# A gated short-convolution block on one core: the output projection as 26 products instead of 7

## The chip, the cores and the metric

The kernel runs on one core of one Trainium2 chip. The metric is the device time of one execution in microseconds (us), from runs of the whole kernel; the profile is one execution taken by the hardware profiler. The engines are TensorE (PE, with its weight load PEld), VectorE (DVE), ScalarE (ACT), GpSimd (POOL) and SyncE (SP), the last of which here only issues transfers.

## What is computed

With x of 1024 rows and 1024 columns, all in float32:

```python
u = rms_norm(x, pre_norm)
z, bg, cg, v = split(u @ w_in, 4)                  # w_in: 1024 x 8192, four parts of 2048
y = bg * causal_dwconv(cg * v, conv_w) * silu(z)   # three taps, 2048 channels
m = y @ w_out                                      # w_out: 2048 x 1024
out = x + rms_norm(m, post_norm)
```

## The kernel before

A float32 product is made of three matmuls in a reduced-width float32 form: each operand is split into a high part (a rounding copy on ScalarE) and a low part (source minus high, on VectorE), and low x high, high x low and high x high are added in PSUM.

The input projection is done in groups of 128 columns. After a first chunk, the remaining 60 groups are taken in 20 triples (numbered 0 to 19). Each triple takes 20 products of block sums (`ORDER`), one after the other, 6 matmuls each; the weights' sums for the next triple are formed on GpSimd meanwhile (`sums`), split (`split_w`), and the products are read from PSUM into the groups (`read`). Convolution and gates follow as soon as their inputs are there (`run_due`), and `y_half` stores each half chunk of y (128 channels by 512 rows) to DRAM in `y_d`.

For the output projection the kernel uses 7 products a, b, c, e, d, f, g of 2x2 blocks. The sums of y that they need are made in DRAM during the main loop: `y_half` stores pieces also to `s_d`, and `more` adds further pieces there by accumulating transfers that GpSimd's queue issues. The sums of w_out are made the same way in `t_d` (`fetch_t`, `add_t`).

In the last stage (from line 908) `fetch_unit` loads 1 MB of y or w, `split_unit` splits it in two pieces of 128x1024 (ScalarE, then VectorE, lines 128 and 129, 851 and 852), `out_mm` runs the matmuls (lines 929 to 931: 4 row tiles q, 4 blocks k, 3 matmuls), and `combine` reads the products from PSUM. `early_half` and `finish_o` do the second normalisation and add x (`norm_square` at line 938, weighing at 953, 968 and 973, the reciprocal root in `rstd_finish` and `rstd_double`, final adds at 979 to 988). GpSimd's part in this stage is four subtractions at line 969 and one short add at the end. 18 buffers of 8 KB per partition (`up`) hold the split operands, 6 of 4 KB (`raw`) the loaded w. Instructions run on each engine in the order in which the program issues them.

Of the kernel before, what the change touches and what calls it, by code (L numbers as in the profile page):

```python
# [20 lines left out]
def kernel(
# [790 lines left out]
    OUT = [(i, h) for i in "abcedfg" for h in (0, 1)]  # L812
    UNITS_O = [(side, i, h) for i, h in OUT for side in "uy"]
    CQ = CH // 2
    fetched, OP = [], {}

    def fetch_unit():
        n = len(fetched)
        if n >= len(UNITS_O):
            return  # L820
        side, i, h = UNITS_O[n]
        js = slice(h * CQ, (h + 1) * CQ)
        far = slice(CH + h * CQ, CH + (h + 1) * CQ)
        if side == "u":
            plain_u = {"a": wov[:, js, :HB], "b": wov[:, far, :HB], "f": wov[:, far, HB:]}
            src = plain_u[i] if i in plain_u else t_d[:, TK[i], js]
            r = []
            for q in (0, 1):
                r.append(raw.tile([P, 2, HB], F32, tag="raw", name=f"r{side}_{i}{h}{q}"))
                nc.sync.dma_start(r[q], src[:, 2 * q : 2 * q + 2])  # L830
        else:
            plain_y = {"a": y_d[:, js, :HB], "b": y_d[:, far, :HB], "g": y_d[:, far, HB:]}
            src = plain_y[i] if i in plain_y else s_d[:, SK[i], js]
            t = up.tile([P, 2, 2, HB], F32, tag="u", name=f"r{side}_{i}{h}")
            nc.sync.dma_start(t.rearrange("p a b c -> p (a b) c"), src)
            r = [t[:, 0], t[:, 1]]
        fetched.append(r)

    def split_unit(delayed=False):
        n = len(OP)  # L840
        if n >= 2 * len(UNITS_O):
            return
        side, i, h = UNITS_O[n // 2]
        q = n % 2
        t = new_u(f"o{side}_{i}{h}{q}")
        src, hi, lo = flat(fetched[n // 2][q]), flat(t[:, 0]), flat(t[:, 1])
        if (side, i) == ("u", "c"):
            nc.scalar.mul(hi, src, -1.0)
            nc.vector.scalar_tensor_tensor(lo, src, -1.0, hi.bitcast(F32), op0=ALU.mult, op1=ALU.subtract)
        elif delayed:  # L850
            nc.scalar.copy(hi, src)
            low_us.append(lambda: nc.vector.tensor_sub(lo, src, hi.bitcast(F32)))
        else:
            split(src, hi, lo)
        OP[side, i, h, q] = t
# [211 lines left out]
```

## Time and profile before

| | |
|---|---|
| time, median of 3 runs | 767.53 us (767.28 to 768.38) |
| profiled execution, span from the first to the last instruction | 766.2 us |
| PE busy | 758.0 us (99%) |
| VectorE, ScalarE, GpSimd busy | 485.9, 452.5, 459.7 us |
| moved by DMA | 116.55 MB, mean 152 GB/s |

The profiled execution's own time is known as its span; the time of a run also has what lies around the span. A row of instructions names the line, the engine, the operation, what is written and read, the shape, then the total busy time and the mean of one, then the idle time just before and what ended it. A row of the timeline begins with start and duration in us.

### The profile page before, as it was taken

The page shows a single profiled execution, that of the slowest core. Times are in us where ns is not written, and L with a number is a line of the kernel's source. Part 1 is how long each engine was busy: PE and PEld are TensorE (multiplying, and loading weights), DVE is VectorE, ACT ScalarE, POOL GpSimd, SP SyncE. Part 2 cuts the span into 40 slices and gives each one's busy share as a digit, 9 for nine tenths or more (in the row PEclk, how much of TensorE's full clock was granted, in tenths as well). Part 3 has the DMA queues.
Part 4 walks back from the last instruction along what each step waited for, and adds up shares of the span by engine and source line. Part 5 has one row for each costly group of instructions (what it writes and reads, how often), then busy time and mean ns, then how long its engine had stood idle before and what let it go on. Part 6 is the DMA issues. An engine that isn't in the chain of part 4 may idle for free.

```text
span 766.2 us, 10006 instructions
## 1 busy us (share of the span) xinstructions
PE 758.0 (99%) x3386; PEld 627.4 (82%) x3386; DVE 485.9 (63%) x748; ACT 452.5 (59%) x881; POOL 459.7 (60%) x564
## 2 busy tenths in 40 slices
PE   9999999999999999999999999999999999999996
PEld 8888888888888888888888888888888888888885
DVE  5898776475656566656565664655566957545755
ACT  8869766557646665754666665666467735544531
POOL 0687979669676876976797796797765220000021
PEclk9999999999999999999999999999999999999999
DMA  9401335447356358165465556574545689754237
GB/s 327 142 1 64 102 97 155 133 110 191 86 154 152 94 116 213 40 183 122 134 153 128 122 151 152 124 182 98 132 97 168 205 281 373 277 189 173 79 123 261
DMA packets 103363, 116.55 MB, mean 152 GB/s; under 512 B 4696, under 2 KB 70544, under 8 KB 102288
## 3 DMA queue, kind: packets, MB, share of 16 engines
q1 hardware_dynamic: 94080, 99.13, 39.4%
q0 software_dynamic: 9216, 16.78, 14.0%
q8 instruction: 26, 0.43, 0.2%
q14 instruction: 25, 0.20, 0.1%
q10 hardware_dynamic: 16, 0.00, 0.0%
HBM read 97.02 MB, written 44.04 MB: 184 GB/s over the span
## 4 chain that ended last, share of the span: by engine, by line
PE 98%; DMA 0%; DVE 0%; ACT 0%; issue 0%; DVEq 0%
PE pX L132 8%; PE pX L134 8%; PE pX L133 8%; PE pY L132 7%; PE pY L134 7%; PE pY L133 7%; PE po_x L931 4%; PE po_x L930 4%; PE po_x L929 4%; PE pV L134 4%; PE pV L132 4%; PE pV L133 4%; PE pZ L134 2%; PE pW L134 2%; PE pW L132 2%; PE pZ L132 2%
## 5 line engine op out<-in xcount | busy, mean ns | idle before, releaser
L362 DVE TENSOR_TENSOR sn<-sn,pY 128x512 f32<-128x512 f32 x57 | 39.2, 687 | 56.4 <-PE pY L134 28.9
L969 POOL TENSOR_TENSOR res<-xr,res 128x512 f32<-128x512 f32 x4 | 6.9, 1736 | 105.4 <-DVE res L968 104.0
L338 POOL TENSOR_TENSOR g<-g,sn 128x512 f32<-128x512 f32 x29 | 40.1, 1390 | 42.2 <-ACT sn L336 35.4
L362 DVE TENSOR_TENSOR sn<-sn,pX 128x512 f32<-128x512 f32 x57 | 39.2, 688 | 33.5 <-PE pX L134 33.5
L311 POOL TENSOR_TENSOR g<-sn,g 128x512 f32<-128x512 f32 x23 | 29.9, 1298 | 47.5 <-DVE sn L360 47.5
L336 ACT ACTIVATE sn<-sn 128x512 f32<-128x512 f32 x24 | 15.2, 632 | 64.1 <-DVE sn L362 40.0
L356 ACT ACTIVATE sn<-pV 128x512 f32<-128x512 f32 x38 | 20.6, 596 | 48.0 <-PE pV L134 48.0
L320 POOL TENSOR_TENSOR g<-g,sn 128x512 f32<-128x512 f32 x20 | 28.2, 1411 | 19.2 <-DVE sn L362 18.9
L354 ACT COPY sn<-pZ 128x512 f32<-128x512 f32 x19 | 11.2, 588 | 46.6 <-PE pZ L134 46.6
L368 POOL DMA_DIRECT2D s_d<-s_d x24 | 19.8, 823 | 21.6 <-DMA s_d<-y_d 14.1
L178 POOL TENSOR_TENSOR raw<-raw 128x256 f32<-128x256 f32 x40 | 32.3, 918 | 0.0
L360 DVE TENSOR_TENSOR g<-pY,g 128x512 f32<-128x512 f32 x15 | 10.4, 692 | 30.7 <-PE pY L134 30.7
L183 POOL TENSOR_TENSOR raw<-e,raw 128x256 f32<-128x256 f32 x40 | 28.7, 739 | 1.6
L179 POOL TENSOR_TENSOR e<-raw,raw 128x512 f32<-128x512 f32 x20 | 26.2, 1312 | 1.6
L938 ACT ACTIVATE jk<-res 128x512 bf16<-128x512 f32 x12 | 7.6, 631 | 31.7 <-DVE res L1008 13.0
L132 PE MATMUL pp<-b,wn 128*128 128x512 f32 x62 | 24.6, 397 | 0.0
L133 PE MATMUL pp<-b,wn 128*128 128x512 f32 x62 | 24.3, 393 | 0.0
L134 PE MATMUL pp<-b,wn 128*128 128x512 f32 x62 | 24.2, 390 | 0.0
L301 DVE SCALAR_TENSOR_TENSOR g<-g,cw,cv 128x512 f32<-128x512 f32 x30 | 22.5, 749 | 1.7
L233 DVE TENSOR_TENSOR wE<-wE,wE 128x512 fp32r<-128x512 f32 x20 | 13.7, 686 | 14.1 <-ACT wE L232 14.0
L301 DVE SCALAR_TENSOR_TENSOR cv<-g,cw,cv 128x512 f32<-128x512 f32 x30 | 22.4, 747 | 0.0
L233 DVE TENSOR_TENSOR wC<-wC,wC 128x512 fp32r<-128x512 f32 x20 | 13.7, 687 | 11.9 <-ACT wC L228 11.9
(388 smaller groups left out, 2903.3 us busy)
## 6 DMA issues: line engine op xcount, KB each, us to landing
raw<-in_sc_w_in SPq DMA_DIRECT2D x64, 512.0 KB, 4.2
t_d<-in_sc_w_out SPq DMA_DIRECT2D x32, 256.0 KB, 4.6
s_d<-g SPq DMA_DIRECT2D x29, 256.0 KB, 2.1
s_d<-s_d POOLq DMA_DIRECT2D x24, 256.0 KB, 4.4
y_d<-g SPq DMA_DIRECT2D x23, 256.0 KB, 2.5
t_d<-in_sc_w_out POOLq DMA_DIRECT2D x16, 256.0 KB, 7.8
t_d<-t_d POOLq DMA_DIRECT2D x16, 256.0 KB, 4.8
xr<-in_x SPq DMA_DIRECT2D x8, 512.0 KB, 5.7
```

What stands on the lines that cost most here:

```text
L132: nc.tensor.matmul(ps, lo, u[:, 0, kk], start=first, stop=False, skip_group_check=True)
L133: nc.tensor.matmul(ps, hi, u[:, 1, kk], start=False, stop=False, skip_group_check=True)
L134: nc.tensor.matmul(ps, hi, u[:, 0, kk], start=False, stop=last, skip_group_check=True)
L178: 0: lambda: (add(w2[:, 0], w2[:, 0], w2[:, 1]), add(w2[:, 2], w2[:, 1], w2[:, 2])),
L183: 5: lambda: (sub(w0[:, 2], e[:, 3], w0[:, 2]), sub(w0[:, 0], e[:, 3], w0[:, 0])),
L301: nc.vector.scalar_tensor_tensor(g if j == TAPS - 1 else ps, g, tap(c, j), ps, op0=ALU.mult, op1=ALU.add)
L311: nc.gpsimd.tensor_mul(g, src, g)
L338: when([(c, "cv", h), (c, "silu", h)], (c, "z", h), {"cv": 1, "silu": 1}, lambda: nc.gpsimd.tensor_mul(cv_of(c, h), cv_of(c, h), t))
L362: nc.vector.tensor_sub(a, a, ps)
L929: nc.tensor.matmul(ps, lo, u[:, 0, k % 2], start=first, stop=False, skip_group_check=True)
L930: nc.tensor.matmul(ps, hi, u[:, 1, k % 2], start=False, stop=False, skip_group_check=True)
L931: nc.tensor.matmul(ps, hi, u[:, 0, k % 2], start=False, stop=last, skip_group_check=True)
```

## The change

The output projection is split as 2 column blocks of w_out by 4 blocks of the 2048 channels by 4 blocks of the rows, and computed by 26 products of sums of blocks instead of 32. A product is named by eight digits (which blocks of w are added), a block of y (0 to 15, or 16 to 19 for a place that holds a sum), the PSUM chain that it is added to, and the output blocks that read the chain after it, with their signs (`PRODUCTS`). A product has two row tiles of 128 and takes 2 x 4 x 3 matmuls.

The sums of w_out are made in DRAM, one in each of the triples 1 to 17 and the rest of two in triple 18 (`MAKES`, `make_w`): a copy of an earlier sum (1 MB, SP) at the triple's product 3, and the block to be added in two accumulating transfers of 512 KB (GpSimd's queue) at products 15 and 20 (5 and 10 for one of triple 18). y goes to DRAM once, without sums. In the last stage all of y is loaded into SBUF, and 30 sums are formed there in place (`ADDS`), 128x1024 each.

An order written out by hand places every step (`PLAN`): a number from -21 to 0 is a product of the last two triples, a number from 1 to 52 a product's row tile of the last stage (2n + q + 1), here called a slot. The steps are F load half of a w sum, Y load y, h high part, l low part, + a sum of y (the last letter d or p says VectorE or GpSimd), r read a chain into an output block (ScalarE for the block's first time, else VectorE), E and L square, e and N and R the reciprocal root, G and H weigh by post_norm, f and o final add and store, X load x, P load post_norm, p last read.

```diff
+PRODUCTS = (
+    ("00000100", 5, "E", {5: 1}),
+    ("01100100", 5, "E", {6: -1}),
+    ("01010000", 4, "A", {0: 1}),
...
+    ("01010100", 17, "F", {1: 1, 2: -1}),
+    ("01010101", 1, "F", {5: -1}),
...
+    ("10000000", 0, "D", {0: 1}),
+    ("01100000", 5, "C", {2: -1}),
+    ("00000001", 14, "C", {}),
+    ("01100110", 10, "C", {6: 1}),
+)
+ADDS = (
+    (16, 3, "+", 1), (17, 7, "-", 16), (5, 5, "+", 17), (6, 10, "-", 6), (5, 6, "-", 5), (4, 4, "-", 8),
+    (3, 11, "-", 3), (3, 11, "-", 16), (18, 5, "+", 9), (18, 3, "+", 18), (18, 4, "-", 17), (19, 1, "-", 18),
+    (17, 13, "+", 17), (1, 1, "-", 13), (12, 12, "-", 4), (9, 12, "+", 17), (19, 0, "+", 19), (19, 19, "-", 8),
+    (15, 15, "-", 7), (13, 12, "-", 15), (11, 13, "-", 11), (6, 17, "-", 6), (8, 2, "-", 8), (12, 14, "-", 12),
+    (12, 12, "+", 17), (13, 2, "-", 13), (0, 0, "-", 2), (10, 10, "-", 2), (8, 8, "+", 10), (5, 5, "-", 8),
+)
+PLAN = {
+    -21: "F",
+    -19: "Y0",
+    -18: "h0.0",
+    -17: "Y1",
+    -16: "l0.0d",
+    -15: "Y2",
+    -13: "+0d Y3",
+    -11: "F",
+    -9: "Y5 +1d",
+    -8: "h0.1",
+    -7: "F +2d",
+    -6: "l0.1p F",
+    -5: "+3d h0.y Y4",
+    -4: "h1.0 l0.yd +6p",
+    -3: "F h1.1",
+    -2: "+4d F",
+    -1: "l1.0p",
+    0: "l1.1d F h1.y",
+    1: "h2.0 l1.yd F h2.1 +5d",
+    2: "l2.0p F r0.0.5 l2.1d h2.y F l2.yd",
+    3: "r0.1.5 +8p h3.y F +27d h3.0 l3.yd F",
+    4: "r1.0.6 l3.0d +7p h3.1 Y6 l3.1d",
+    5: "r1.1.6 h4.0 +9d Y7 h4.1 l4.0d",
+    6: "r2.0.0 l4.1p h4.y +14d F l4.yd",
+    7: "r2.1.0 F h5.0 +10d +18p h5.1 F +11d",
+    8: "r3.0.3 l5.0d h5.y F l5.1p l5.yd F",
+    9: "r3.1.3 +12d h6.y +13p F h6.0 l6.yd",
+    10: "P r4.0.1 l6.0d h6.1 +15p F l6.1d",
+    11: "r4.1.1 +16d F h7.y +19p h7.0 l7.yd",
+    12: "r5.0.4 l7.0d h7.1 +17p F l7.1d",
+    13: "r5.1.4 +20d F h8.y +21p h8.0 l8.yd",
+    14: "h8.1 r6.0.5 l8.0d l8.1p +23d F",
+    15: "h9.y r6.1.5 h9.0 +24p F l9.yd h9.1",
+    16: "r7.0.1 r7.0.2 l9.0d l9.1p +26d F",
+    17: "r7.1.2 r7.1.1 h10.y F h10.0 l10.yd",
+    18: "h10.1 l10.0p r8.0.5 l10.1d F",
+    19: "h11.y r8.1.5 h11.0 l11.yd F h11.1 l11.0d",
+    20: "X X l11.1p r9.0.5 F E1.0",
+    21: "h12.y r9.1.5 F h12.0 l12.yd h12.1 l12.0d",
+    22: "r10.0.7 l12.1d F E1.1 e1.0 e1.1 G1.0 F",
+    23: "r10.1.7 G1.1 h13.y h13.0 l13.yd",
+    24: "h13.1 l13.0p r11.0.4 l13.1d F",
+    25: "h14.y r11.1.4 h14.0 l14.yd F h14.1 l14.0d",
+    26: "l14.1p r12.0.1 F",
+    27: "h15.y r12.1.1 F h15.0 l15.yd h15.1 l15.0d +25p",
+    28: "r13.0.3 F l15.1d",
+    29: "h16.y r13.1.3 F h16.0 l16.yd h16.1 l16.0d",
+    30: "l16.1p r14.0.7 F",
+    31: "h17.y r14.1.7 F h17.0 l17.yd h17.1 l17.0d +22p",
+    32: "r15.0.3 F r15.0.7 l17.1d E3.0",
+    33: "h18.y r15.1.3 F r15.1.7 h18.0 l18.yp e3.0 G3.0 E3.1",
+    34: "r16.0.1 h18.1 e3.1 G3.1 L1.0 l18.1p l18.0d",
+    35: "R1.0 h19.y r16.1.1 F N1.0 L1.1 l19.yp H1.0 F R1.1 h19.0",
+    36: "r17.0.4 h19.1 N1.1 H1.1 E0.0 l19.0p f1.0",
+    37: "h20.y r17.1.4 o1.0 E0.1 f1.1 l19.1p F o1.1",
+    38: "r18.0.3 l20.yd L3.0 +28p F R3.0",
+    39: "h21.y r18.1.3 N3.0 L3.1 H3.0 l21.yp R3.1 H3.1 h21.0",
+    40: "r19.0.0 h21.1 N3.1 f3.0 l21.0p",
+    41: "h22.y r19.1.0 o3.0 h22.0 f3.1 l21.1p F h22.1 o3.1",
+    42: "r20.0.2 e0.0 e0.1 G0.0 l22.yp F G0.1",
+    43: "h23.0 r20.1.2 l22.0d h23.1 +29p l22.1d F",
+    44: "r21.0.2 F l23.0d l23.1p h23.y",
+    45: "r21.1.2 h24.y l23.yd h24.0 l24.yd h24.1",
+    46: "l24.0p r22.0.0 l24.1d L0.0 R0.0",
+    47: "h25.y r22.1.0 N0.0 L0.1 l25.yp H0.0 R0.1 H0.1 h25.0",
+    48: "r23.0.2 h25.1 N0.1 l25.0p E2.0 f0.0",
+    49: "r23.1.2 o0.0 E2.1 l25.1p f0.1 o0.1",
+    50: "p0 e2.0 e2.1 G2.0 G2.1",
+    51: "p1",
+    52: "L2.0 H2.0 R2.0 N2.0 f2.0 L2.1 H2.1 o2.0 R2.1 N2.1 f2.1 o2.1",
+}
+
+MAKES = {
+    1: (("01000100", "01000000", "00000100"),),
+    2: (("01010000", "01000000", "00010000"),),
+    3: (("01100100", "01000100", "00100000"),),
...
+    17: (("00001110", "00001100", "00000010"),),
+    18: (("00001101", None, "00000001"), ("11110000", None, "10000000")),
+}
+PARTIAL = {"00001100": "00001101", "01110000": "11110000"}
...
-    CH = NC // 2
-    SK = {"c": 0, "e": 1, "f": 2, "d": 3}
-    TK = {"d": 0, "e": 1, "g": 2, "c": 3}
+    KP = NC // 4
+    KB = KP // 2
+    QT = L // 4
+    sums_w = sorted({f for f, _, _, _ in PRODUCTS if f.count("1") > 1})
     y_d = dram.tile([P, NC, L], F32, tag="y_d", name="y_d")
-    s_d = dram.tile([P, 4, CH, HB], F32, tag="s_d", name="s_d")
-    t_d = dram.tile([P, 4, CH, HB], F32, tag="t_d", name="t_d")
+    t_d = dram.tile([P, len(sums_w), KP, HB], F32, tag="t_d", name="t_d")
...
     def y_half(c, h, cv):
...
+        nc.sync.dma_start(y_d[:, c, h * HB : (h + 1) * HB], cv)
+    def w_blocks(f, ks):
+        if f.count("1") > 1:
+            return t_d[:, sums_w.index(PARTIAL.get(f, f)), ks]
+        i, k = divmod(f.index("1"), 4)
+        return wov[:, k * KP + ks.start : k * KP + ks.stop, i * HB : (i + 1) * HB]
+    def make_w(t, s):
+        for n, (f, of_f, add) in enumerate(MAKES.get(t, ())):
+            if of_f and s == 3:
+                nc.sync.dma_start(w_blocks(f, slice(0, KP)), w_blocks(of_f, slice(0, KP)))
+            at = (15, 20) if of_f or n else (5, 10)
+            if s in at:
+                ks = slice(at.index(s) * KB, (at.index(s) + 1) * KB)
+                more(w_blocks(f, ks), w_blocks(add, ks))
...
+    p2, place = [], {}
+    halves = [(n, k) for n, (f, *_) in enumerate(PRODUCTS) for k in range(2) if n < 2 or f != PRODUCTS[n - 2][0]]
+    loaded, ops, chains, given = {}, {}, {}, set()
+    WE = {n: n - 2 for n in range(2, len(PRODUCTS)) if PRODUCTS[n][0] == PRODUCTS[n - 2][0]}
+    def block_y(r):
+        if r // 2 not in place:
+            place[r // 2] = up.tile([P, KP, HB], F32, tag="u", name=f"y_{r // 2}")
+        return place[r // 2][:, :, r % 2 * QT : (r % 2 + 1) * QT]
+    def load_y(n):
+        k, h = divmod(n, 2)
+        block_y(2 * n)
+        nc.sync.dma_start(place[n], y_d[:, k * KP : (k + 1) * KP, h * HB : (h + 1) * HB])
+    def load_w():
+        n, k = halves[len(loaded)]
+        t = loaded[n, k] = raw.tile([P, KB, HB], F32, tag="raw", name=f"rw_{n}{k}")
+        nc.sync.dma_start(t, w_blocks(PRODUCTS[n][0], slice(k * KB, (k + 1) * KB)))
+    def add_y(n, eng):
+        d, a, op, b = ADDS[n]
+        (eng.tensor_add if op == "+" else eng.tensor_sub)(block_y(d), block_y(a), block_y(b))
+    def operand(n, u):
+        t = ops[n, u]
+        if u == "y":
+            return block_y(PRODUCTS[n][1]), *(t[:, z].rearrange("p a (b l) -> p (a b) l", b=2) for z in (0, 1))
+        return loaded[n, int(u)], t[:, 0], t[:, 1]
+    def high_o(n, u):
+        ops[n, u] = new_u(f"o{u}_{n}")
+        src, hi, _ = operand(n, u)
+        nc.scalar.copy(hi, src)
+    def low_o(n, u, eng):
+        src, hi, lo = operand(n, u)
+        eng.tensor_sub(lo, src, hi.bitcast(F32))
...
+    def run_plan(at):
+        for step in PLAN.get(at, "").split():
+            what, arg = step[0], step[1:].rstrip("dp")
+            eng = nc.gpsimd if step[-1] == "p" else nc.vector
+            if what == "F":
+                load_w()
+            elif what == "Y":
+                load_y(int(arg))
+            elif what == "+":
+                add_y(int(arg), eng)
+            elif what in "hl":
+                n, u = arg.split(".")
+                high_o(int(n), u) if what == "h" else low_o(int(n), u, eng)
+            else:
+                LATE[what](*(int(n) for n in arg.split(".") if n))
...
+            make_w(t, s)
+            if t >= END - 1:
+                run_plan((t - END) * len(ORDER) + s - len(ORDER))
...
+    def out_mm(n, q):
+        _, _, ch, _ = PRODUCTS[n]
+        first = ch not in chains or q == 1 and chains[ch] == n
+        if first:
+            chains[ch] = n
+            out_banks[ch, q] = bank(f"po_{ch}{q}")
+        ps = out_banks[ch, q]
+        y = operand(n, "y")[1:]
+        for k in range(KP):
+            w = ops[WE.get(n, n), str(k // KB)]
+            hi, lo = (y[z][:, k, q * P : (q + 1) * P] for z in (0, 1))
+            nc.tensor.matmul(ps, lo, w[:, 0, k % KB], start=first and k == 0, stop=False, skip_group_check=True)
+            nc.tensor.matmul(ps, hi, w[:, 1, k % KB], start=False, stop=False, skip_group_check=True)
+            nc.tensor.matmul(ps, hi, w[:, 0, k % KB], start=False, stop=k == KP - 1, skip_group_check=True)
...
+    for n in range(len(PRODUCTS)):
+        for q in range(2):
+            out_mm(n, q)
+            run_plan(2 * n + q + 1)
+    tail["store"]()
```

More of the change, by code (lines that the diff above doesn't have):

```diff
@@ L209 @@
     }
-    lows, low_us = [], []
+    lows = []
     def run_lows():
@@ L810, in first_chunk @@
             gate_y(0, 1, plain_ps[3, 1], 1, True)
[L812 to L855, printed above, removed]
+    p2, place = [], {}
@@ L918 @@
-    ob = {}
-    def out_mm(i, h, q):
-        which = i if i == "b" else "v" if i in "ef" else "x"
-        if (which, q) not in ob:
-            ob[which, q] = bank(f"po_{which}{q}")
-        ps = ob[which, q]
-        for k in range(CQ):
-            u, y = OP["u", i, h, k // 2], OP["y", i, h, k // 2]
-            hi, lo = (y[:, z, k % 2, q * P : (q + 1) * P] for z in (0, 1))
-            first, last = i in "abe" and h == 0 and k == 0, h == 1 and k == CQ - 1
-            nc.tensor.matmul(ps, lo, u[:, 0, k % 2], start=first, stop=False, skip_group_check=True)
-            nc.tensor.matmul(ps, hi, u[:, 1, k % 2], start=False, stop=False, skip_group_check=True)
-            nc.tensor.matmul(ps, hi, u[:, 0, k % 2], start=False, stop=last, skip_group_check=True)
@@ L1033 @@
-    finish_row(TH - 1)
-    assert len(OP) == 2 * len(UNITS_O)
-    for q in range(TH):
-        for h in (0, 1):
-            out_mm("g", h, q)
-        if q == TH - 1:
-            ob["last"] = ob["v", q][:, : HB - CUT]
-            nc.scalar.copy(ob["last"], C22[:, q, CUT:])
-        combine("g", q)
-        finish_row(q + TH)
+    so_all = small.tile([P, SMALL], F32, tag="so_all", name="so_all", bufs=1)
+    out_banks, done_rows, rows_in, tail = {}, [], [], {}
+    TP = PRODUCTS[-1][3]
+    (last_block, last_sign), = TP.items()
@@ new lines, in weigh, with sum_early @@
+    def weigh(t, q, late):
+        j = block_at(t, late)
+        o, sign, to = res_of(j, q), 1, res_of(j, q)
+        if j == last_block:
+            o, sign = out_banks[PRODUCTS[-1][2], q], last_sign
+            if q == 1:
+                to = tail["z"] = bank("z_last")
+        nc.vector.scalar_tensor_tensor(to, o, -0.5 * sign, gpost[:, half_cols(j)], op0=ALU.mult, op1=ALU.mult)
+    def sum_early(t, q):
+        nc.vector.tensor_scalar(so_all[:, row(t, q) : row(t, q) + 1], so[:, row(t, q), :1], EPS, None, op0=ALU.add)
@@ new lines, in root, with newton @@
+    def root(t, q):
+        sd = small.tile([P, 1], F32, tag="sd1", name=f"sd_post{t}{q}")
+        r = row(t, q)
+        nc.scalar.activation(sd, so[:, r, 1:], AF.Sqrt, bias=so_all[:, r : r + 1])
+        fin[t, q] = sd
+        if (t, q) == (LAST_T, 1):
+            tail["e"] = bank("e_last")[:, : HB - CUT]
+            nc.scalar.copy(tail["e"], res_of(block_at(t, 0), q)[:, CUT:])
+    def newton(t, q):
+        r = row(t, q)
+        fin[t, q] = rstd_double(fin[t, q], so[:, r, 1:], f"post{t}{q}", so_all[:, r : r + 1])
@@ new lines @@
+    ROWS = [(int(s[1]), int(s[3])) for at in sorted(PLAN) for s in PLAN[at].split() if s[0] == "o"]
+    LATE.update(
+        P=lambda: nc.sync.dma_start(gpost, post_norm.broadcast_to([P, D])),
+        X=load_res,
+        r=read_out,
+        p=to_bank,
+        E=lambda t, q: square_o(t, q, 0),
+        e=sum_early,
+        G=lambda t, q: weigh(t, q, 0),
+        L=lambda t, q: square_o(t, q, 1),
+        R=root,
+        H=lambda t, q: weigh(t, q, 1),
+        N=newton,
+        f=lambda t, q: finish_half(t, q, 1),
+        o=lambda t, q: finish_half(t, q, 0),
+    )
```

254 lines of the change are left out of this document (97 added, 157 removed).

## The prediction

> **What bounds the kernel now.** I read four views, in this order: the page's busy line with the chain that ended last, the windows of the output stage, the TensorE rows of that stage, and the timeline of VectorE and GpSimd around its start.
>
> ```profile
> PE 758.0 (99%) x3386; PEld 627.4 (82%) x3386; DVE 485.9 (63%) x748; ACT 452.5 (59%) x881; POOL 459.7 (60%) x564
> PE 98%; DMA 0%; DVE 0%; ACT 0%; issue 0%; DVEq 0%
> 300.00:580.00 280.00, 280.00 (x1237) 231.82 (x1236) 168.76 (x256) 165.17 (x345) 216.32 (x274) 1.00 0.54 128
> 607.00:642.00 35.00, 35.00 (x156) 28.98 (x155) 22.91 (x21) 20.00 (x24) 7.73 (x7) 1.00 0.79 258
> 677.00:712.00 35.00, 35.00 (x156) 28.96 (x156) 17.55 (x18) 14.98 (x20) 0.00 (x0) 1.00 0.62 234
> 712.00:747.00 35.00, 35.00 (x156) 29.00 (x155) 23.59 (x47) 15.14 (x29) 5.15 (x3) 1.00 0.21 74
> ```
>
> The window rows give length, then busy time of PE, weight load, VectorE (DVE), ScalarE (ACT) and GpSimd (POOL), the granted clock and the DMA share. PE never stops, so every matmul costs its full time, and no other engine's time counts. In the output stage GpSimd is nearly or wholly idle and VectorE is half to two thirds busy. That idle GpSimd is the cover that the change spends.
>
> **The matmuls that go.** The output stage has 7 products x 2 halves x 4 row tiles x 4 blocks x 3 passes = 672 matmuls; the new one has 26 products x 2 row tiles x 4 blocks x 3 = 624, of the same 128x128 by 128x512 shape.
>
> ```profile
> L931 PE MATMUL po_x<-ou_a,oy_a x32: 389/389/389, 607.5 to 628.5; 128*128 128x512 f32 x32
> ...
> L931 PE MATMUL po_x<-ou_g,oy_g x32: 388/389/389, 738.0 to 759.1; 128*128 128x512 f32 x32
> ```
>
> One L931 matmul ends each group of three; there are 224. From the first to the last start are 759.1 - 607.5 = 151.6 us and 223 x 3 = 669 steps, so one matmul takes 0.2266 us of PE (389 ns is its length in the pipeline). 48 fewer are -10.9 us. One "slot" of the new stage (a product for one row tile, 12 matmuls) is 2.72 us, and a product 5.44 us. This gain holds only if the operands are ready in time.
>
> **What the operands cost.** Each operand is split into a high part (ScalarE) and a low part, source minus high, both in SBUF. There are 26 y operands and 50 halves of w (one w is used twice), so 76 splits of 128x1024 where there were 56, and 30 new y sums of the same size. The plan marks 50 low parts and 16 sums for VectorE, 26 low parts and 14 sums for GpSimd. All of these read two SBUF tensors. What happens when both engines do that is seen where the old stage begins:
>
> ```profile
> 590.23 1.30 POOL L311 TENSOR_TENSOR g<-sn,g 128x512 f32<-128x512 f32 x1 [6.63 <-DVE sn L360]
> 590.67 1.94 DVE L852 TENSOR_TENSOR ou_a<-ru_a,ou_a 128x1024 fp32r<-128x1024 f32 x1
> 594.93 1.21 DVE L852 TENSOR_TENSOR ou_a<-ru_a,ou_a 128x1024 fp32r<-128x1024 f32 x1
> 596.06 0.67 DVE L362 TENSOR_TENSOR sn<-sn,pY 128x512 f32<-128x512 f32 x1
> 603.00 1.30 POOL L311 TENSOR_TENSOR g<-sn,g 128x512 f32<-128x512 f32 x1 [2.27 <-DVE sn L360]
> 603.43 1.95 DVE L852 TENSOR_TENSOR ou_a<-ru_a,ou_a 128x1024 fp32r<-128x1024 f32 x1
> 611.77 1.22 DVE L852 TENSOR_TENSOR oy_a<-ry_a,oy_a 128x1024 fp32r<-128x1024 f32 x1
> 612.00 2.15 POOL L338 TENSOR_TENSOR g<-g,sn 128x512 f32<-128x512 f32 x1 [3.14 <-ACT ou_b L128]
> ```
>
> The low part at 594.93 ran with GpSimd quiet: 1.21 us, and the next instruction started 1.13 us after it. The one at 590.67 began inside a GpSimd multiply that ended at 591.53, and ended at 592.61, that is 1.08 us after GpSimd was done; the one at 603.43 ended 1.08 us after GpSimd's end at 604.30. The other way round, the GpSimd multiply at 612.00 began inside a low part that ended at 612.99 and ended at 614.15, 1.16 us later, though alone it takes 1.30. So the two do not share, they take turns: whichever comes second stands still until the first has finished. VectorE instructions with a PSUM operand do not wait:
>
> ```profile
> L362 DVE TENSOR_TENSOR sn<-sn,pY 128x512 f32<-128x512 f32 x57 | 39.2, 687 | 56.4 <-PE pY L134 28.9
> L953 DVE SCALAR_TENSOR_TENSOR res<-res,gpost 128x512 f32<-128x512 f32 x8 | 5.5, 692 | 6.7 <-ACT jk L938 6.7
> L988 DVE SCALAR_TENSOR_TENSOR res<-res,rs_post,xr 128x512 f32<-128x512 f32 x7 | 5.2, 747 | 0.2 <-DMA xr<-in_x 0.2
> 64.81 3.81 POOL L590 TENSOR_TENSOR u<-s,u 128x512 fp32r<-128x512 f32 x3
> 73.92 1.43 POOL L178 TENSOR_TENSOR raw<-raw 128x256 f32<-128x256 f32 x2
> ```
>
> L362 runs through the main loop, where GpSimd is busy 216 of 280 us, at 687 ns. So what must take turns is: all GpSimd sums and low parts, and VectorE's sums, low parts, weighing by gpost and final adds (both operands SBUF), not its reads of PSUM.
>
> **Prices.** VectorE 128x1024: 1.13 us (from 1.08, behind a wait, to 1.22). GpSimd 128x1024 does not occur. Three of 128x512 took 3.81 us, 1.27 each; two of 128x256 took 1.43, 0.72 each; 0.55 us per 256 columns gives 2.38 for 1024. Below: 2 x 1.16 less 0.17 of fixed time (0.72 - 0.55) = 2.15; above: 2 x 1.30 = 2.60. I take 2.38, since back-to-back rows carry it. A weighing is 0.69, a final add 0.75, and the tiny reciprocal-root steps with two SBUF operands I put at 0.4 a row tile as an estimate.
>
> [...]
>
> **The sum, by stretches of 13 slots (35.4 us of PE each), counted from the plan.**
> Slots 1 to 13: VectorE 17 low parts and 9 sums, 26 x 1.13 = 29.4; GpSimd 3 and 8, 11 x 2.38 = 26.2; together 55.6 us.
> Slots 14 to 26: 16 x 1.13 = 18.1; 7 x 2.38 = 16.7; 2 weighings 1.4; 36.1 us.
> Slots 27 to 39: 10 x 1.13 = 11.3; 10 x 2.38 = 23.8; 6 weighings 4.1; 4 final adds 3.0; small 1.2; 43.4 us.
> Slots 40 to 49: 6 x 1.13 = 6.8; 9 x 2.38 = 21.4; 4 weighings 2.8; 6 final adds ahead of the last low part 4.5; small 1.2; 36.7 us.
> Sum 171.8 us of taking turns before the last product can start, which PE would like to start after 50 slots = 136.0 us. PE must therefore wait 35.8 us in all. The lead with which the stage starts is in the sum already: I count nothing listed at or before slot 0, which is 8 VectorE and 3 GpSimd pieces, 16.2 us, in the 22 us from slot -16 on, beside the last gating multiplies. No larger lead can build up: the operands rotate through 18 buffers of which 9 hold y, so at most three products are held.
>
> Together: -10.9 + 35.8 = +24.9 us. The profiled execution has a span of 766.2 us, 1.3 us below the median of the runs, 767.5; I put that 1.3 on both. So 766.2 + 24.9 + 1.3 = 792.4 us.
>
> Ends of the unknown prices: with 1.08 and 2.15 the turns are 58 x 1.08 + 37 x 2.15 + 18.2 = 160.4, a wait of 24.4, and 781.0 us. On the other side, VectorE's 36 reads of PSUM (0.6 each, 22 us) need no turn but stand in the same queue: if none falls under a GpSimd instruction, the wait is 57 us and the time 814. I take none of it, since a read often stands next to a GpSimd piece in a slot, and keep 814 for the range.
>
> **What stays covered.** ScalarE: 70 high parts, 16 first reads, 16 squares.
>
> ```profile
> L128 ACT CAST ou_d<-ru_d 128x1024 fp32r<-128x1024 f32 x4 | 4.0, 1050 | 0.0
> L1001 ACT COPY res<-po_x 128x512 f32<-128x512 f32 x4 | 2.4, 589 | 10.9 <-PE po_x L931 10.9
> L938 ACT ACTIVATE jk<-res 128x512 bf16<-128x512 f32 x12 | 7.6, 631 | 31.7 <-DVE res L1008 13.0
> s_d<-s_d POOLq DMA_DIRECT2D x24, 256.0 KB, 4.4
> t_d<-in_sc_w_out POOLq DMA_DIRECT2D x16, 256.0 KB, 7.8
> ry_b<-y_d SPq DMA_DIRECT2D x2, 1024.0 KB, 9.9
> ```
>
> 70 x 1.05 + 16 x 0.59 + 16 x 0.63 = 93 us of 141: covered at any PE pace. Loads in the stage: 50 of 512 KB and 8 of 1 MB, 33 MB against 28 MB, over a longer stage; hidden, and if one is late it delays a stage that is late already.
>
> The main loop loses 64 GpSimd-issued accumulating transfers of 256 KB and gets 38 of 512 KB, 19 MB for 16, and 17 DRAM copies of 1 MB on SP for 32 stores and 32 fetches of 256 KB. A copy waits at product 3 for the sum issued at product 20 before, about 4 us earlier; that lands after perhaps 8 to 16 us (twice 4.4 to 7.8), so SP stands up to 12 us, with the y stores queued behind it. The sum at product 15 comes 12 x 1.36 = 16.3 us after product 3; a copy that starts late and takes 9.9 us could hold GpSimd's queue some 5 us. GpSimd has (280 - 216) / 280 x 27.2 = 6 us free in each triple, so I take 0; if the wait were 2 us longer than that in all 17 triples, +34. The gain side is nothing, since PE has no wait there. The tail after the last matmul (759.5 to 766.2) keeps its kinds of step: 0, give or take 2.
>
> **The rivals.**
> *Cover holds, PE stays the bound.* If GpSimd and VectorE overlapped freely, each engine would fit: VectorE 29.4 of 35.4 us in the first stretch, GpSimd 26.2. Then the time is 767.5 - 10.9 = 756.6, faster. It decides as soon as the taking turns costs less than 136 us for the 50 slots, which at 1.13 needs a GpSimd piece of 1.4 us, nearly the price of half its size. Against it stand three VectorE rows and one GpSimd row that waited to the end of the other.
> *Partly covered.* The order of the pieces could let early low parts run further ahead than I count; with the low prices and 8 us of lead the wait is 16 and the time 773.
> *The wait also slows the clock.* After the last matmul the granted clock falls:
>
> ```profile
> 758.00:760.00 2.00, 1.50 (x7) 0.92 (x5) 1.67 (x4) 0.47 (x1) 0.00 (x0) 1.00 0.88 293
> 760.00:762.00 2.00, 0.00 (x0) 0.00 (x0) 1.64 (x6) 0.90 (x4) 0.00 (x0) 1.00 0.90 350
> 762.00:764.00 2.00, 0.00 (x0) 0.00 (x0) 0.90 (x2) 0.02 (x1) 0.45 (x1) 0.67 0.40 139
> 764.00:766.20 2.20, 0.00 (x0) 0.00 (x0) 0.00 (x0) 0.00 (x0) 0.00 (x0) 0.50 0.31 119
> ```
>
> PE ended at 759.5; a mean of 0.67 over 762 to 764 puts the step to 0.50 at about 762.7, 3.2 us into the idle time. In products 2 to 9 the turns come to about 9 us a product, a gap of 3.6 us; if every such gap halved the clock for the next product, it would take 10.9 us in place of 9, 8 x 1.9 = 15 us more: 807. [...]
>
> **How the numbers follow.** A difference of 0.2% is about what a measurement of this kernel tells from none. Forecast (781 to about 800): 0.63. Clock slowed or the reads not overlapped (800 to 815 and beyond): 0.16. Partly covered (766 to 781): 0.11, of which 0.02 is within 0.2%. Free overlap: 0.10, faster. So faster 0.10, same 0.02, slower 0.88. The range 773 to 812 leaves out the free overlap and the far tail.
>
> **What would show it.** Right: PE idle of 25 to 60 us in the output stage, half of it within the first 17 slots, ended by low parts of VectorE or GpSimd; VectorE 128x1024 instructions with a mean near 2 us in place of 1.22; GpSimd 128x1024 spans well above 2.4; 624 matmuls at 0.227 us spacing between the waits. Wrong: 128x1024 pieces of both engines running over each other at their own length, PE at 99% again, or waits that end on transfers or in the main loop.

## The result and the profile after

The changed kernel takes 834.53 us (median of 4 runs, 830.94 to 836.23) where the kernel before takes 767.5: a ratio of 1.0863, 95% interval 1.0838 to 1.0887. It is slower, as forecast, but by 67 us where 25 were forecast. The profiled execution has a span of 829.2 us and is the fastest of the four, 830.94. These are its busy line, the start of the chain that ended last, and the windows (columns as before: length, PE, weight load, VectorE, ScalarE, GpSimd, granted clock, DMA share, GB/s).

```profile
PE 777.0 (94%) x3338; PEld 625.3 (75%) x3338; DVE 581.3 (70%) x784; ACT 474.9 (57%) x904; POOL 562.2 (68%) x574
PE 79%; DVE 13%; issue 3%; DMA 2%; ACT 1%; POOL 1%; SPq 0%; DVEq 0%; POOLq 0%
300.00:580.00 280.00, 280.00 (x1201) 225.60 (x1201) 164.21 (x249) 162.63 (x340) 207.66 (x255) 1.00 0.58 143
607.00:642.00 35.00, 24.71 (x98) 19.33 (x97) 28.61 (x27) 13.42 (x19) 21.49 (x11) 0.87 0.71 263
642.00:677.00 35.00, 31.29 (x122) 25.12 (x121) 34.93 (x18) 20.70 (x27) 21.56 (x8) 0.89 0.70 234
677.00:712.00 35.00, 22.58 (x89) 17.36 (x88) 35.00 (x22) 13.04 (x15) 22.94 (x8) 0.90 0.44 135
712.00:747.00 35.00, 33.91 (x150) 27.79 (x149) 33.57 (x32) 20.16 (x25) 14.89 (x6) 1.00 0.65 214
782.00:817.00 35.00, 22.93 (x90) 17.81 (x89) 32.89 (x43) 10.40 (x17) 18.17 (x7) 0.85 0.42 144
```

Three things differ from before. First, PE is idle for 829.2 - 777.0 = 52.2 us, where it was idle for 766.2 - 758.0 = 8.2: +44.0. Of the 52.2, 50 lie after 607 (7.3 of them behind the last matmul, where the kernel before has 6.7), and there VectorE is the full engine: 69.93 of the 70 us from 642 to 712. Second, PE's busy time rose by 19.0 us although it has 48 matmuls fewer. A part of that is the granted clock, 0.85 to 0.90 in the four windows in which PE loses most. Third, from 300 to 580, where PE never waits and the clock is 1.00, 1201 matmuls start where 1237 did. A matmul of the main loop takes 280 / 1201 = 0.2331 us; it took 280 / 1237 = 0.2264.

The groups of the two new kinds of work (`add_y` is line 939, the low parts are line 954), and the transfers that GpSimd issues:

```profile
L954 POOL TENSOR_TENSOR o<-rw,o 128x1024 fp32r<-128x1024 f32 x21 | 60.4, 2880 | 40.3 <-ACT o L950 27.1
L939 POOL TENSOR_TENSOR y<-y,y 128x1024 f32<-128x1024 f32 x14 | 44.2, 3161 | 27.4 <-DVE oy L954 16.2
L504 POOL DMA_DIRECT2D t_d<-in_sc_w_out x38 | 44.7, 1177 | 0.0
L954 DVE TENSOR_TENSOR o<-rw,o 128x1024 fp32r<-128x1024 f32 x29 | 57.8, 2007 | 0.0
L954 DVE TENSOR_TENSOR oy<-y,oy 128x1024 fp32r<-128x1024 f32 x21 | 35.9, 1712 | 1.1 <-ACT oy L950 1.1
L939 DVE TENSOR_TENSOR y<-y,y 128x1024 f32<-128x1024 f32 x16 | 32.2, 2012 | 4.4 <-DMA y<-y_d 4.3
```

VectorE's low parts of w and its sums have a mean of 2.0 us, its low parts of y 1.71; one that nothing holds up is 1.21. Rows from the timeline of the two engines show why (first number the start, second the duration; the rows of GpSimd carry POOL):

```profile
631.19 2.42 POOL L954 TENSOR_TENSOR o<-rw,o 128x1024 fp32r<-128x1024 f32 x1
...
655.87 1.21 DVE L954 TENSOR_TENSOR o<-rw,o 128x1024 fp32r<-128x1024 f32 x1
656.08 3.27 POOL L939 TENSOR_TENSOR y<-y,y 128x1024 f32<-128x1024 f32 x1 [1.22 <-DMA y<-y_d]
657.00 3.42 DVE L939 TENSOR_TENSOR y<-y,y 128x1024 f32<-128x1024 f32 x1
659.49 3.14 POOL L954 TENSOR_TENSOR o<-rw,o 128x1024 fp32r<-128x1024 f32 x1
660.35 3.35 DVE L954 TENSOR_TENSOR oy<-y,oy 128x1024 fp32r<-128x1024 f32 x1
```

Read the ends. VectorE's low part ends at 657.08; GpSimd's sum, begun at 656.08, ends at 659.35, 2.27 later; VectorE's next piece, begun at 657.00, ends at 660.42, 1.07 after that; GpSimd's next ends at 662.63, 2.21 later; VectorE's next at 663.70, 1.07 later. They run one after the other: a pair costs 3.3 us, in which one VectorE piece and one GpSimd piece get done.

What PE and its suppliers waited for (total, times, longest):

```profile
ACT res L1044 <- DMA y_d<-g: 7.1, 1, 7.1
DVE y L939 <- DMA y<-y_d: 4.3, 1, 4.3
ACT res L1046 <- DVE res L1048: 16.0, 1, 16.0
PE po_D L1035 <- DVE res L1048: 10.6, 1, 10.6
PE po_F L1035 <- ACT res L1046: 7.9, 1, 7.9
PE po_E L1035 <- ACT res L1044: 7.0, 1, 7.0
PE po_F L1036 <- DVE o L954: 4.4, 2, 2.7
PE po_B L1035 <- DVE oy L954: 3.7, 1, 3.7
PE pY L268 <- DVE sn L498: 3.3, 1, 3.3
```

The two longest waits of PE, 10.6 and 7.9 us, are not for an operand. PE wants a PSUM chain again whose last value VectorE has not read, or has read so late that ScalarE's read behind it is late too (line 1046, which stood 16.0 us for line 1048): VectorE's reads stand in the queue behind the pieces that take turns. Two more come from the start of the stage. VectorE stood 4.3 us in its queue for a load of y, with the main loop's last reads behind it. And ScalarE's first read into `res` stood 7.1 us, because `res` lies in memory out of which the last store of y (`y_d<-g`) was still leaving.

### The profile page after: what moved, and what is told of

It reads as the page before. It is cut to its first block, busy times and chain, and to the rows that moved or that the text cites. A ratio compares the mean times of both kernels' runs of the same rounds, so it can differ in the third digit from the quotient of the medians.

```text
span 829.2 us, 10012 instructions
## 1 busy us (share of the span) xinstructions
PE 777.0 (94%) x3338; PEld 625.3 (75%) x3338; DVE 581.3 (70%) x784; ACT 474.9 (57%) x904; POOL 562.2 (68%) x574
## 4 chain that ended last, share of the span: by engine, by line
PE 79%; DVE 13%; issue 3%; DMA 2%; ACT 1%; POOL 1%; SPq 0%; DVEq 0%; POOLq 0%
PE pX L269 8%; PE pX L270 8%; PE pX L268 8%; PE pY L268 7%; PE pY L270 7%; PE pY L269 7%; PE pV L269 3%; PE pV L268 3%; PE pV L270 3%; DVE y L939 3%; DVE o L954 3%; PE pW L269 2%; PE pZ L269 2%; PE pW L270 2%; PE pZ L270 2%
## 5 line engine op out<-in xcount | busy, mean ns | idle before, releaser
L954 POOL TENSOR_TENSOR o<-rw,o 128x1024 fp32r<-128x1024 f32 x21 | 60.4, 2880 | 40.3 <-ACT o L950 27.1
L950 ACT CAST o<-rw 128x1024 fp32r<-128x1024 f32 x50 | 50.9, 1048 | 24.9 <-DMA rw<-in_sc_w_out 17.1
L939 POOL TENSOR_TENSOR y<-y,y 128x1024 f32<-128x1024 f32 x14 | 44.2, 3161 | 27.4 <-DVE oy L954 16.2
L954 DVE TENSOR_TENSOR o<-rw,o 128x1024 fp32r<-128x1024 f32 x29 | 57.8, 2007 | 0.0
L504 POOL DMA_DIRECT2D t_d<-in_sc_w_out x38 | 44.7, 1177 | 0.0
L950 ACT CAST oy<-y 128x1024 fp32r<-128x1024 f32 x26 | 27.1, 1046 | 22.6 <-DVE y L939 13.5
L954 DVE TENSOR_TENSOR oy<-y,oy 128x1024 fp32r<-128x1024 f32 x21 | 35.9, 1712 | 1.1 <-ACT oy L950 1.1
L314 POOL TENSOR_TENSOR raw<-raw 128x256 f32<-128x256 f32 x40 | 36.0, 1106 | 0.0
L939 DVE TENSOR_TENSOR y<-y,y 128x1024 f32<-128x1024 f32 x16 | 32.2, 2012 | 4.4 <-DMA y<-y_d 4.3
L268 PE MATMUL pp<-b,wn 128*128 128x512 f32 x62 | 24.6, 397 | 0.0
L269 PE MATMUL pp<-b,wn 128*128 128x512 f32 x62 | 24.3, 393 | 0.0
## 6 DMA issues: line engine op xcount, KB each, us to landing
y<-y_d SPq DMA_DIRECT2D x8, 1024.0 KB, 10.2
```

Of the source, the lines that this page charges most:

```text
L268: nc.tensor.matmul(ps, lo, u[:, 0, kk], start=first, stop=False, skip_group_check=True)
L269: nc.tensor.matmul(ps, hi, u[:, 1, kk], start=False, stop=False, skip_group_check=True)
L314: 0: lambda: (add(w2[:, 0], w2[:, 0], w2[:, 1]), add(w2[:, 2], w2[:, 1], w2[:, 2])),
L504: nc.gpsimd.dma_start(dst, src, accum_op=ALU.add)
L939: (eng.tensor_add if op == "+" else eng.tensor_sub)(block_y(d), block_y(a), block_y(b))
L954: eng.tensor_sub(lo, src, hi.bitcast(F32))
```

## The experiments

Time is split below into PE's idle time (span minus busy) and its busy time, both from the page of each run. The first can be laid to waits, the second to what one matmul takes.

| kernel | median us | ratio, 95% interval | PE idle | PE busy |
|---|---|---|---|---|
| before | 767.5 | 1 | 8.2 | 758.0 |
| after | 834.5 | 1.0863 [1.0838, 1.0887] | 52.2 | 777.0 |
| e5_undo | 817.1 | 1.0642 [1.0617, 1.0667] | 51.1 | 764.3 |
| e4_poolwrites | 784.6 | 1.0223 [1.0207, 1.0238] | 15.8 | 766.1 |
| e5b_undo_pw | 769.7 | 1.0026 [1.0016, 1.0037] | 16.6 | 751.2 |
| c1_alld | 792.6 | 1.0320 [1.0303, 1.0337] | 32.2 | 758.8 |
| c2a_starts | 789.1 | 1.0271 [1.0255, 1.0286] | 29.5 | 757.9 |
| c2b_mixed | 795.4 | 1.0360 [1.0343, 1.0378] | 35.8 | 757.0 |

### What makes a matmul of the main loop longer?

The diff has two lines that I had priced at nothing, since they compute the same: two tiles of 32 bytes per partition go to another pool.

```diff
-    sq = small.tile([P, NT], F32, tag="sq", name="sq", bufs=1)
-    gcol = small.tile([P, NK], F32, tag="gcol", name="gcol", bufs=1)
+    sq = snp.tile([P, NT], F32, tag="sq", name="sq", bufs=1)
+    gcol = snp.tile([P, NK], F32, tag="gcol", name="gcol", bufs=1)
```

`small` lies ahead of the buffers of u (`up`), which the main loop's matmuls stream as their moving operand; `snp` lies between them and the split weights (`wp`), the stationary operand. From u to the weights there were 194816 bytes per partition, a multiple of 256, and now there are 194880, 64 more. Either the absolute place matters, or this distance, or neither and the cause is the new work in the main loop.

**Everything moved by 32 bytes, in the kernel before and in the kernel after.**

```diff
+    const.tile([P, 8], F32, tag="pad", name="pad")
```

> The kernel before, with 32 unused bytes per partition ahead of all operand buffers, so that they begin at 32 instead of 0 modulo 64, as they do in the changed kernel. Theory A (the changed kernel's matmuls come 0.2333 us apart in the main loop instead of 0.2267 because its operand buffers lie 32 bytes off): all 3386 matmuls lose 0.0066 us, 22 us, so about 790 us, with the longer spacing in every stage. Rival B (the longer spacing comes from the changed kernel's transfers in the main loop): 767.5 us, no change.

> The changed kernel with 32 unused bytes ahead of its operand buffers, which brings them back to 0 modulo 64 (64 modulo 128). Theory A: the spacing is 0.2267 us again; the main loop and the head (2700 matmuls) give back 18 us, in the last stage it is partly hidden by the waits: 812 to 817 us. If the boundary were 128, or by rival B: 834.5 us.

In the kernel before (e1_shift) this gives 768.46 us, 1.0008 [0.9998, 1.0017], and 1237 matmuls from 300 to 580. In the kernel after (e2_align) it gives 833.16 us, 1.0856 [1.0828, 1.0883], and 1202 matmuls. The absolute place is not the cause.

**The weights' side alone moved, in the kernel before.** e1w_shift_w puts the same 32 bytes at the start of `snp`, so that the weights' sums, the groups and the split weights move and u does not; e6_w128 puts 128 bytes there; e7_w_only puts 32 at the start of `wp`, which moves the split weights and little else.

```diff
+    snp.tile([P, 8], F32, tag="pad", name="pad")     # e1w_shift_w; [P, 32] in e6_w128
+    wp.tile([P, 8], F32, tag="pad", name="pad")      # e7_w_only
```

> The kernel before, with the 32 unused bytes behind the 18 shared buffers and the loaded weights: the moving operands of all matmuls stay at 0 modulo 64, the split weights of the main loop, which are the stationary operands, lie at 32. If A holds and the stationary operand makes it: some 2400 matmuls of the main loop lose 0.0066 us, about 783 us. If the moving operand makes it: 767.5 us. Rival B: 767.5 us as well.

> The kernel before, with 128 unused bytes between the buffers of the moving operand and the split weights. Distances of 32 and 64 gave 0.2333 us a matmul. If the rule goes by 128 bytes: 0.2267 us and 767.5 us. If it goes by 256 or more: 0.2333 us and 783.5 us.

> The kernel before, with 32 unused bytes ahead of the split weights alone; the weights' sums and the collected groups, which also moved in e1w_shift_w, stay in place. Distance theory (moving operand to split weights decides): 0.2333 us a matmul and 783.5 us. Rival (one of the other buffers that moved makes it): 767.5 us.

e1w_shift_w takes 783.54 us, 1.0206 [1.0191, 1.0221]; e6_w128 takes 781.62 and e7_w_only 783.23 (one run each). The window from 300 to 580 of e7_w_only:

```profile
300.00:580.00 280.00, 280.00 (x1202) 225.45 (x1201) 164.21 (x250) 162.68 (x340) 214.74 (x272) 1.00 0.54 129
```

and of e6_w128:

```profile
300.00:580.00 280.00, 280.00 (x1207) 226.98 (x1206) 164.81 (x251) 163.70 (x343) 215.85 (x274) 1.00 0.54 129
```

The old kernel, with no line of its work changed, shows the new kernel's pace, 1202 in place of 1237, as soon as the split weights stand 32 bytes further off. With 128 bytes it is nearly as slow, 1207. So it is the distance between the two operands, and of the distances tried (0, 32, 64 and 128 bytes beyond a multiple of 256) only 0 is fast.

**The two lines undone in the kernel after.**

```diff
-    sq = snp.tile([P, NT], F32, tag="sq", name="sq", bufs=1)
-    gcol = snp.tile([P, NK], F32, tag="gcol", name="gcol", bufs=1)
+    sq = small.tile([P, NT], F32, tag="sq", name="sq", bufs=1)
+    gcol = small.tile([P, NK], F32, tag="gcol", name="gcol", bufs=1)
```

> The changed kernel with one part undone: the two small tiles sq and gcol (64 bytes together) are back in the pool ahead of the operand buffers, so that the split weights lie at 194816 bytes (0 modulo 256) behind the buffers of the moving operand, as before the change, instead of 194880. Distance theory (the spacing of matmuls hangs on the distance of the two operands, not on either place): spacing 0.2267 us in the main loop, 16 us less, 815 to 820 us. Rival (it hangs on something else in the changed program): 834.5 us.

It takes 817.12 us, 17.4 less than after, as expected (the two profiled executions differ by 13.8, as that of after was its fastest run). Its window:

```profile
300.00:580.00 280.00, 280.00 (x1237) 231.83 (x1236) 168.84 (x256) 165.39 (x346) 211.77 (x259) 1.00 0.60 145
```

The 20 triples have 20 x 20 x 6 = 2400 matmuls, and 2400 times 0.2331 - 0.2264 make 16.1 us. Making the shift in the old kernel cost 16.0; undoing it in the new one gave 17.4, in which the waits and the clock of the last stage also differ. The last stage is not touched by this: from 650 to 680 e7_w_only starts 134 matmuls, as many as before. In the last stage both operands lie in buffers of 8 KB of one pool, at distances that are multiples of 256.

### What do the turns cost, and who pays?

**GpSimd only writes.** Its 14 sums and 26 low parts (21 of w, 5 of y) become fills of the same tiles, so that these sums and low parts are left out; first beside the slow distance (e4_poolwrites, which also has the 32 bytes of e2_align ahead of everything), then with it undone (e5b_undo_pw).

```diff
+        if eng is nc.gpsimd:
+            nc.gpsimd.memset(block_y(d), 0.5)
+            return
...
+        if eng is nc.gpsimd:
+            nc.gpsimd.memset(lo.bitcast(F32), 0.0)
+            return
```

> As the run before (32 bytes ahead), and each of GpSimd's 14 sums and 26 low parts is replaced by a fill of the same piece with a constant, so that GpSimd reads no SBUF there; those sums and low parts are left out of the computation. Turn-taking theory: VectorE's 58 pieces of the stage take 1.13 us each and no longer 2, its work is 58 x 1.13 + 36 x 0.6 + 27 = 115 us against 141 us of PE, so PE is the bound and the time is 757 to 766 us. Rival (the waits come from the order of the steps, late loads and buffers): the same steps wait in the same places, 800 us or more.

> As e5_undo, and GpSimd's sums and low parts replaced by fills, as in e4_poolwrites (left out of the computation). If the distance and the turn-taking are separate terms, it is e4_poolwrites less 16 us: 768 to 770 us, with only the two waits at the start of the stage left (3.3 and 3.9 us) and the slow clock after them. If they hide each other: 775 us or more.

They take 784.63 and 769.74 us. The first missed its 757 to 766, because it still had the 16 us of spacing and two waits at the start of the stage. The groups of e4_poolwrites:

```profile
L959 POOL MEMSET o<- 128x1024 f32 x21 | 19.9, 956 | 35.8 <-PE po_F L1044 20.8
L961 DVE TENSOR_TENSOR o<-rw,o 128x1024 fp32r<-128x1024 f32 x29 | 35.2, 1219 | 1.7 <-ACT o L954 1.6
```

VectorE's same 29 pieces take 1219 ns in place of 2007, beside a GpSimd that issues as many instructions into the same tiles. The waits of PE that are left in e5b_undo_pw are the two of the start:

```profile
PE po_E L1041 <- ACT res L1050: 4.0, 1, 4.0
PE pY L268 <- DVE sn L498: 3.7, 1, 3.7
```

So it is what the fills leave out, GpSimd's reading of its operands, and not its instructions, its writes or its semaphores, that stops VectorE: 2007 ns beside the real pieces, 1219 beside the fills. The two parts of the loss add up to within 3 us: e5_undo minus e5b_undo_pw is 47.4 us for GpSimd's real pieces, e4_poolwrites minus e5b_undo_pw 14.9 for the distance, where after minus e5_undo gave 17.4.

The second run also shows what a wait costs beyond itself. PE's timeline there:

```profile
618.18 0.39 PE L1043 MATMUL po_E<-o,oy 128*128 128x512 f32 x1
622.57 0.50 PE L1041 MATMUL po_E<-o,oy 128*128 128x512 f32 x1 [4.00 <-ACT res L1050]
...
623.72 0.63 PE L1041 MATMUL po_E<-o,oy 128*128 128x512 f32 x1
624.14 0.63 PE L1042 MATMUL po_E<-o,oy 128*128 128x512 f32 x1
624.57 0.63 PE L1043 MATMUL po_E<-o,oy 128*128 128x512 f32 x1
...
626.54 0.39 PE L1042 MATMUL po_E<-o,oy 128*128 128x512 f32 x1
626.77 0.40 PE L1043 MATMUL po_E<-o,oy 128*128 128x512 f32 x1
```

After 4.0 us without work the matmuls start 0.43 us apart until 626.28, 3.7 us behind the first of them (622.57), and then return to 0.23. That is the return of the clock: in the profile after, where the steps behind such a wait go from 0.43 to 0.23 us at 704.67, the granted clock is 0.50 from 704.0 to 704.5 and 1.00 from 705.0 to 705.5.

**All on VectorE.** e5_undo with the 40 steps marked p marked d, so that GpSimd does none of them.

```diff
-    7: "r2.1.0 F h5.0 +10d +18p h5.1 F +11d",
-    8: "r3.0.3 l5.0d h5.y F l5.1p l5.yd F",
+    7: "r2.1.0 F h5.0 +10d +18d h5.1 F +11d",
+    8: "r3.0.3 l5.0d h5.y F l5.1d l5.yd F",
...
```

> As e5_undo, with all 40 steps that the plan gives to GpSimd given to VectorE. Turn-taking theory: nothing waits for GpSimd any more; VectorE has 95 pieces of 1.13, 36 reads of 0.6, weighing, final adds and small steps, 107 + 22 + 27 = 156 us ahead of product 25, against 136 us of PE: 20 us of waits and some 7 at the stage's start, 780 to 787 us, faster than e5_undo by 30 us although VectorE has 40 pieces (45 us) more. Rival (VectorE is the bound by its own work, and GpSimd relieves it): slower than e5_undo, 850 us.

It takes 792.60 us, 24.5 less than e5_undo, though VectorE got 40 pieces more. It missed its 780 to 787 and came out far from the 850 of its rival.

```profile
L954 DVE TENSOR_TENSOR o<-rw,o 128x1024 fp32r<-128x1024 f32 x50 | 61.1, 1241 | 0.0
650.00:680.00 30.00, 23.40 (x93) 18.82 (x92) 30.00 (x30) 14.42 (x17) 0.00 (x0) 0.89 0.52 165
PE po_E L1035 <- ACT res L1044: 7.4, 1, 7.4
PE po_F L1035 <- ACT res L1046: 6.6, 1, 6.6
PE po_D L1035 <- DVE res L1048: 4.3, 1, 4.3
PE pY L268 <- DVE sn L498: 3.8, 1, 3.8
```

50 pieces now take 61.1 us where 29 took 57.8. While it takes its turn, a GpSimd piece stops VectorE for 2.2 us, and VectorE would have done the same piece in 1.13. With GpSimd out of it VectorE is full by its own work from 650 to 680 (30.00 of 30), and the time stays 25 us above before; that the one makes the other is argued here, and the next run bears on it.

**VectorE's peak flattened, the two starts eased.** This is c1_alld with seven sums moved from slots 3 to 15 into slots 16 to 23 (the expectation says eight), the first sum four products later and the second one product later (the third stays where it was), and `res` as eight tiles in place of one.

```diff
-    13: "r5.1.4 +20d F h8.y +21d h8.0 l8.yd",
+    13: "r5.1.4 F h8.y h8.0 l8.yd",
...
-    18: "h10.1 l10.0d r8.0.5 l10.1d F",
+    18: "h10.1 l10.0d r8.0.5 l10.1d F +20d",
...
-    res = p2.tile([P, 2 * NE * 4, HB], F32, tag="res", name="res")
+    res = {j: p2.tile([P, 2, HB], F32, tag=f"res{j}", name=f"res{j}") for j in (5, 6, 0, 3, 1, 4, 2, 7)}
```

> As c1_alld, with three edits against the waits that its trace shows: the first three sums of y stand about four products later, when their loads have landed (PE waited 3.8 us); the output blocks are eight tiles instead of one, so that the first read does not wait for the last store of y out of the memory below (7.4 us); eight sums that nothing needs early stand later, in slots 16 to 23. If these waits were causes: 792.6 less 11 and less 3 to 6 of slow clock, 775 to 780 us. Rival (VectorE's 156 us of work is the bound and the waits only its places): 788 to 793 us.

It takes 789.11 us: the rival was right, 788 to 793. The wait of 7.4 us on `res` became one of 3.1 on VectorE's low part, and the main loop's wait of 3.8, for which the first sums were moved, became one of 4.9. The wait that was eased at one place came back at another that VectorE supplies, and from 650 to 680 VectorE is as full as it was:

```profile
650.00:680.00 30.00, 27.32 (x119) 21.99 (x118) 30.00 (x30) 14.87 (x19) 0.00 (x0) 1.00 0.65 212
```

**Twelve low parts of slots 20 to 49 back on GpSimd**, where VectorE also has reads of PSUM, which need no turn (all 36 of the profile after, lines 1048 and 1050, take 0.67 to 0.69 us).

```diff
-    26: "l14.1d r12.0.1 F",
+    26: "l14.1p r12.0.1 F",
...
```

> As c2a_starts, with 12 low parts of slots 20 to 49 back on GpSimd, where VectorE has reads of PSUM that need no turn. If the reads run under them: VectorE's own work falls by 12 x 1.13 = 14 us to about 142 us, 766 to 772 us. If each GpSimd piece only holds VectorE for 2.2 us: 12 x (2.2 - 1.13) = 13 us more than c2a_starts.

It takes 795.42 us, 6.3 more than c2a_starts: not the gain to 766 to 772, and half of the loss that the other branch gave.

```profile
L954 POOL TENSOR_TENSOR o<-rw,o 128x1024 fp32r<-128x1024 f32 x12 | 31.8, 2660 | 123.3 <-ACT o L950 71.3 <-DVE o L954 52.1
L954 DVE TENSOR_TENSOR o<-rw,o 128x1024 fp32r<-128x1024 f32 x38 | 50.6, 1343 | 0.0
```

The 12 pieces cost 0.5 us each. There was no room there: in c2a_starts VectorE is busy 29.18 of the 30 us from 710 to 740 and 29.46 of those from 740 to 770. So a turn of GpSimd costs VectorE more than the piece that it is spared. None of these versions comes below the kernel before.

## Why the prediction was wrong, point by point

**The sign and its cause held.** The turns were taken as the chosen rows of before said, and they decide: without GpSimd's reads, and with the distance undone, the kernel is at 769.7. The free overlap, 756.6, did not happen. The price of a turn was 2.2 us (2.21 and 2.27 in the timeline) where 2.38 was taken; a piece that GpSimd began first is 2.42 (631.19). Of the signs, the idle time of the stage came (40 us, 23 of them in the first 17 slots), and so did VectorE's mean near 2 us and GpSimd's spans of 2.9 and 3.2; but PE's longest waits ended on reads of PSUM and not on low parts.

**The 48 matmuls** went as counted, 3386 to 3338. But "one matmul takes 0.2266 us" was read off the last stage of before and silently taken for every stage of the new kernel. That is the first step that failed: there was no term and no rival for a matmul that gets longer where nothing of its work changes. The runs put 16.0 to 17.4 us in its place, from a distance that grew by 64 bytes. With it the forecast would have been about 809. It does not account for the whole miss: e5_undo, which does not have it, still takes 817.1, above the 812 at which the range ended.

**The turns' sum, 35.8 us, measured 47.4** (e5_undo against e5b_undo_pw; a fill is also shorter than a real piece, 0.96 us against 2.9). Of these 47.4, PE's idle time is 51.1 - 16.6 = 34.5, close to the 35.8. Part of that is luck: with 2.21 to 2.27 in place of 2.38 the prediction's own sum gives 30 to 32. VectorE's reads of PSUM, which the sum let fall under GpSimd's pieces at no cost, may be the rest, since the two longest waits of PE, 10.6 and 7.9 us, end on such reads; no run tried them alone. The other 13.1 us are longer busy time of PE, and here is the second step that failed: the slowed clock stood as a rival to the forecast, and came true beside it. In the profile after, the five longest waits of PE are 3.4, 3.9, 7.2, 8.1 and 10.8 us (from start to start, less one step), and behind each the granted clock is 0.50 for a time in which 6 to 12 whole steps take 0.43 us. The steps in these stretches, those of the waits left out, are together 10.1 us above 0.2267 each; 15 had been the rival's price. Counted in the same way the lowered clock costs 12.6 us in e5_undo and 3.3 in e5b_undo_pw, so 9.3 of the 13.1. No run tried the clock by itself.

**The start of the stage** was counted as free lead. That is the third step that failed. It had two waits that the sum has no place for, each about 4 us in e5b_undo_pw: a sum queued on VectorE ahead of its load, and `res` in memory that a store still read. These, 16.6 - 8.2 = 8.4 us of idle time, with some 3 us of slowed clock behind them, are most of what keeps e5b_undo_pw at 769.7 and not at 757.

**What was called covered was covered.** The main loop has no wait between 300 and 580; the 38 accumulating transfers (1177 ns each on GpSimd) cost it nothing there. ScalarE is at 10 to 22 of 35 us throughout, and its waits are for others. After the two waits at the start, PE's long waits end on VectorE's work and on reads of PSUM, not on loads.

**The sum, as measured.** By the profiles it is -10.9 for the matmuls, 16 to 17 for the distance, 44.0 more idle time and 10.1 for the clock, together 59 to 60; the spans differ by 63.0, and the rest is not accounted for. By the runs, the 42.1 us between 792.4 and 834.5 are 17.4 for the distance (after to e5_undo), 11.6 for the turns with their slow clock (47.4 in place of 35.8) and 13.1 for what is left without both (769.7 in place of 756.6). The upper end of the turns was taken without the clock, and there was no term for the distance or the start, so the range ended at 812.

## What to carry to other kernels

Before a piece of work goes to an idle GpSimd, see whether VectorE is doing anything with two SBUF operands at that time: here 40 pieces moved back to a fuller VectorE made the kernel 24.5 us faster. In a diff, look also at the lines that only move tiles between pools, and compare the spacing of matmuls in a stretch that the change should leave alone: it is the first reading that separates a wait from a slower matmul. And count a wait of PE with the slow matmuls that may follow it, about 2 us more for each of the five here, of 3.4 to 10.8 us.

## What the hardware showed that was not expected

The pace of a matmul of 128x128 by 128x512 depended on where its two operands lie to each other in SBUF. With the split weights at a multiple of 256 bytes from the moving operand 1237 started in 280 us, at 32 or 64 bytes beyond it 1201 or 1202, at 128 beyond it 1207, with no wait and the clock at 1.00 in all of them. Which part of the chip this comes from, and what other distances do, the runs do not show. The fall of the clock did not come at a fixed time after the last matmul: PE stopped at 692.40 + 0.39 = 692.79 in the profile after, and the windows put the step near 697.8, 5 us later, where the end of the kernel before showed 3.2. Nor did the length of the wait alone decide: a wait of 2.4 us in e5_undo (behind the matmul at 667.66) was followed by slow matmuls, and one of 3.0 us in the profile after (behind the one at 682.11) was not. The five stretches of lowered clock ahead of the last matmul of that profile last 3.4, 10.2, 3.4, 6.8 and 10.2 us (from the granted clock in windows of 0.5 us): one, two or three times the shortest. The last matmul ahead of that wait in the timeline, and the windows behind it:

```profile
692.40 0.39 PE L1037 MATMUL po_F<-o,oy 128*128 128x512 f32 x1
700.70 0.80 PE L1035 MATMUL po_F<-o,oy 128*128 128x512 f32 x1 [7.91 <-ACT res L1046]
```

```profile
694.00:696.00 2.00, 0.00 (x0) 0.00 (x0) 2.00 (x3) 0.00 (x0) 0.01 (x1) 1.00 0.23 55
696.00:698.00 2.00, 0.00 (x0) 0.00 (x0) 2.00 (x2) 0.00 (x0) 2.00 (x1) 0.95 0.71 253
698.00:700.00 2.00, 0.00 (x0) 0.00 (x0) 2.00 (x3) 0.00 (x0) 2.00 (x2) 0.50 0.00 1
```
